# The single-token step of a hybrid decoder layer: eight sequences in one pass, outputs written in place by the products

## The chip, the cores and the metric

The kernel runs on one core of one Trainium2 chip, in one launch. The metric is the device time of the launch in microseconds (us). The time of before is the median of three runs.

## What is computed

Two layers of a decoder. Every layer normalises x, projects it with one large matrix (`w_in`, 3,200 columns in 25 tiles of 128), runs three groups of causal recurrences on the result, gates them and projects back (`w_out`). Two sets of sequences go through the same weights: one prompt of 1,024 tokens, and eight sequences of a single new token each, which bring their own states. The kernel lays both side by side as 1,032 columns (`NT`), the last eight being the single tokens.

The part that concerns us is the single-token step of two of the groups, HGRN2 ("A", six heads, keys of 64) and GLA ("B", six heads, keys of 32), values of 64 each. For every sequence b and head h:

```python
S_new = f[:, None] * S + k[:, None] * v[None, :]   # (K, V)
o     = S_new.T @ q                                # (V,)
```

`S_new` is an output of the kernel, and `o` goes on to a norm over the head, a gate and `w_out`.

## The kernel before

**The large products.** `gemm_tile` (it calls `mm`, L156, the line of every product by `mm`) takes one tile of weights through three blocks of columns (384, 384, 264). Each float32 operand is split into a high and a low part, and each of 8 steps of the contraction makes three products of single-pass type (`wh*hh`, `wh*lo`, `wl*hh`). Weights come in halves of a tile (`raw`, two buffers, 256 KB each, L270 on SyncE's queue), are rounded by ScalarE (`wh`, L146) and subtracted by VectorE or GpSimd in turn (`wl`, L289).

**The rest is woven between them.** Python generators (`unit_a`, `unit_b`, `s5_thread`, `decode` and others) are advanced by `tick()` inside `gemm_tile`; this sets the program order. Tile's scheduler then lays out each engine's order from dependencies and a timeline of its own, when the kernel is built. Each engine, and SyncE's queue (SP), runs its own order strictly: what waits at the head holds up all behind it.

**The single-token step.** `turn` (L856 to L860) transposes the last eight columns of a value tile, ScalarE copies them into `vd` (8 sequences by 128), and a DMA puts them into `vdd` in DRAM, 8 rows of 768. `decode` (L919 to L958) runs five times a layer: B0 (four heads), B1 (two heads, 64 rows), A0, A1, A2 (two heads each), one behind the other by `dec_lock`. A decode

- clears `qbd` (GpSimd, L923) and copies each head's queries into its own column (VectorE, L925);
- in two halves of four sequences: loads the states `dS` (L930) and, one DMA a head, the values broadcast over the head's rows into `dV` (L932); GpSimd makes `dS*f`, `dV*k` and their sum (L935 to L937); SP stores the new states (L939). `dS` has two buffers, `dV` one, so the second half's values are loaded when the first half's sum is done;
- makes eight products with `qbd` as the weights (128x32) and a sequence's states as 64 columns; the outputs lie by sequence and head, so ScalarE copies them to SBUF, TensorE transposes them (L950), ScalarE copies again into `dO`, and two small DMAs a head (64 runs of 16 bytes, L956) carry them to `odec`, rows by head and value.

Each call of `psum("aux")` takes one of two banks that the other threads use too. Much later `dec_norm` reads `odec` (L1377).

What surrounds it on the engines: in `unit_a`, GpSimd multiplies `qs` by `ep` (L985), and VectorE's scans (L874) write over `ep` behind that; `headnorm` on VectorE makes `sl` (L908), on which TensorE waits. In `s5_thread`, GpSimd makes `s5W` (L575 to L580).

Of the kernel before, what the change touches and what calls it, by code (L numbers as in the profile page):

```python
# [8 lines left out]
F32 = mybir.dt.float32  # L9
F32R = mybir.dt.float32r  # L10
I8 = mybir.dt.int8
AF = mybir.ActivationFunctionType
ALU = mybir.AluOpType

P = 128
# [23 lines left out]
def tile_hybrid_step(ctx: ExitStack, tc: tile.TileContext, a: dict, nl=NL, limit=RANGE):  # L39
    nc = tc.nc  # L40
    V, S, G, TE, SY = nc.vector, nc.scalar, nc.gpsimd, nc.tensor, nc.sync

    cst = ctx.enter_context(tc.tile_pool(name="cst", bufs=1))
# [6 lines left out]
    dram = ctx.enter_context(tc.tile_pool(name="dram", bufs=1, space=bass.MemoryType.DRAM))  # L50
# [7 lines left out]
    def nm(s):  # L58
        cnt[0] += 1
        return f"{s}_{cnt[0]}"  # L60
# [16 lines left out]
    def release(x):  # L77
        t = tag_of.pop(id(x))
        del owner[t]
        free.append(t)  # L80

    def psum(tag, shape=(P, 512), dt=F32):
        n = {"g": 2, "att": 1, "o": 2, "aux": 2}[tag]
        return ps.tile(list(shape), dt, tag=tag, bufs=n, name=nm("ps_" + tag))

    def tmp(tag, shape, dt=F32, bufs=1):
        return tp.tile(list(shape), dt, tag=tag, bufs=bufs, name=nm(tag))
# [57 lines left out]
    def act(out, in_, func, **kw):  # L145
        return S.activation(out=out, in_=in_, func=func, **kw)  # L146
# [8 lines left out]
    def mm(out, lhsT, rhs, start=True, stop=True):  # L155
        return TE.matmul(out=out, lhsT=lhsT, rhs=rhs, start=start, stop=stop)  # L156
# [8 lines left out]
    ident = cst.tile([P, P], F32, name="ident")  # L165
# [12 lines left out]
    epsc = cst.tile([P, 1], F32, name="epsc")  # L178
    V.memset(epsc, EPS)
    atts = [cst.tile([P, 2, 2, P], F32, name=f"atts{i}") for i in range(2)]  # L180
    hh = big.tile([P, KD, NT], F32R, name="hh")
    def blocks(dt):

        return [big.tile([P, KD, n], dt, tag=f"lo{b}", name=nm("lo")) for b, (o, n) in enumerate(BLK)]
# [188 lines left out]
    def s5_prep(l, d):  # L373
# [81 lines left out]
        V.tensor_tensor(out=t1, in0=t1, in1=t2, op=ALU.subtract)  # L455
        V.tensor_tensor(out=ci, in0=t1, in1=rd, op=ALU.mult)

        ts = tmp("dV", [P, 4, 64]).rearrange("p a b -> p (a b)")
        bc = lambda x: x.unsqueeze(2).to_broadcast([P, 8, 16])
        cmul(G, bb[:, 0], bb[:, 1], s5w[:, 0], s5w[:, 1], bc(cr), bc(ci), ts[:, :128].rearrange("p (a b) -> p a b", b=16))  # L460
        yield
# [193 lines left out]
    def prep(l):  # L655
        s5["d"] = {}
        s5["th"] = spawn(s5_prep(l, s5["d"]))


    def layer(l, slow=False):  # L660
# [19 lines left out]

        usd = dram.tile([2, P, 8, P], F32, name=nm("usd"))
        udd = dram.tile([2, P, 8], F32, name=nm("udd"))
        vdd = dram.tile([8, 768], F32, name=nm("vdd"))
        st, onorm = {}, {}

        if l == 0:
            masks()
            prep(0)
# [112 lines left out]
        for b in range(3):  # L801
            o, n = BLK[b]
            p = psum("o")
# [5 lines left out]
            x = rbT[:, o:o + n]  # L809
# [27 lines left out]
        def values(w0, part):  # L837
            vt = big.tile([P, 3 * NT], F32, tag=f"vx{part}", name=nm("v"))[:, :3072].rearrange("p (c f) -> p c f", f=384)
            for i in range(3):
                room(1)  # L840
                f = alloc("vf", [P, NT])
                gemm_tile(wt[w0 + i], [0, 1, 2], hrhs, ev_copy(f))
                spawn(turn(vt, f, part, i))
            return vt

        def turn(vt, f, part, i):
            for h in range(2):
                p = psum("aux")
                for c in range(4):
                    t0 = (4 * h + c) * P  # L850
                    TE.transpose(out=p[:, c * P:(c + 1) * P], in_=f[:, t0:t0 + P], identity=ident)  # L851
                act(out=vt[:, 4 * h:4 * h + 4, i * P:(i + 1) * P], in_=p.rearrange("p (c f) -> p c f", f=P),
                    func=AF.Copy)
                yield
            p = psum("aux")
            TE.transpose(out=p[:8, :P], in_=f[:, T:NT], identity=ident)  # L856
            vd = tmp("vd", [8, P])
            act(out=vd, in_=p[:8, :P], func=AF.Copy)
            SY.dma_start(out=vdd[:, part * 384 + i * P:part * 384 + (i + 1) * P], in_=vd)
            release(f)  # L860
            turned[part] += 1


        odec = lay.tile([P, 6, 8], F32, tag="odec", name=nm("odec"))
# [54 lines left out]
        def decode(pr, nh, kd, f8, k8, q8, head0, u0, sin, sout):  # L919

            yield from dec_lock.take()
            qbd = tmp("qbd", [P, 8, 32])[:pr]
            G.memset(qbd, 0.0)  # L923
            for h in range(nh):
                V.tensor_copy(out=qbd[h * kd:(h + 1) * kd, :, h], in_=q8[h * kd:(h + 1) * kd, :])  # L925
            sbs = []
            for b0 in (0, 4):
                sb = tmp("dS", [P, 4, 64], bufs=2)[:pr]
                vb = tmp("dV", [P, 4, 64])[:pr]
                SY.dma_start(out=sb, in_=sin[:, b0:b0 + 4, :])  # L930
                for h in range(nh):
                    SY.dma_start(out=vb[h * kd:(h + 1) * kd], in_=vdd[b0:b0 + 4, (head0 + h) * 64:(head0 + h) * 64 + 64]  # L932
                                 .unsqueeze(0).to_broadcast([kd, 4, 64]))
                yield
                G.tensor_tensor(out=sb, in0=sb, in1=f8[:, b0:b0 + 4].unsqueeze(2).to_broadcast([pr, 4, 64]), op=ALU.mult)  # L935
                G.tensor_tensor(out=vb, in0=vb, in1=k8[:, b0:b0 + 4].unsqueeze(2).to_broadcast([pr, 4, 64]), op=ALU.mult)
                G.tensor_tensor(out=sb, in0=sb, in1=vb, op=ALU.add)  # L937
                yield
                SY.dma_start(out=sout[:, b0:b0 + 4, :], in_=sb)  # L939
                sbs.append(sb)  # L940
            yield

            po = psum("aux")
            for i, sb in enumerate(sbs):
                for b in range(4):
                    mm(po[32 * b:32 * b + 32, 64 * i:64 * i + 64], qbd[:, 4 * i + b, :], sb[:, b, :])
            stg = tmp("dV", [P, 4, 64]).rearrange("p a b -> p (a b)")[:, :P]
            act(out=stg, in_=po[:, :P], func=AF.Copy)
            po = psum("aux")
            TE.transpose(out=po[:, :P], in_=stg, identity=ident)  # L950
            stg = tmp("dO", [P, 4, 4])[:, :nh]
            act(out=stg, in_=po[:, :P].rearrange("p (b h) -> p h b", h=32)[:, :nh], func=AF.Copy)
            for h in range(nh):
                u, hf = divmod(h, 2)
                for i in range(2):
                    SY.dma_start(out=odec[64 * hf:64 * hf + 64, u0 + u, 4 * i:4 * i + 4], in_=stg[64 * i:64 * i + 64, h, :])  # L956
            dec_lock.give()
            decodes[0] += 1  # L958

# [548 lines left out]
    def masks():  # L1508

        for i, m in enumerate((maskA, maskB, maskD)):  # L1510
            mk = tmp("dV", [P, 4, 64]).rearrange("p a b -> p (a b)")[:, :P]
            SY.dma_start(out=mk, in_=a["c_mask"][:, i])
            V.tensor_copy(out=m, in_=mk[:, :m.shape[1]])

# [114 lines left out]
```

## Time and profile before

| | |
|---|---|
| median of the runs | 1073.71 us |
| runs | 1069.07, 1073.71, 1224.8 us |
| the profiled execution, its own time | 1070.87 us |
| its span | 1068.8 us |
| busy: TensorE, VectorE, ScalarE, GpSimd | 94%, 60%, 46%, 44% |
| mean granted TensorE clock | 0.972 of full |

The share of TensorE is high because matmuls are pipelined and the record of each one covers its latency. In the profile's names PE is TensorE, PEld its weight loads, DVE VectorE, ACT ScalarE, POOL GpSimd, SPq the queue from which SyncE issues the DMAs. `<-` names what an instruction waited for last. L156 is the line of the helper that issues every product.

### The profile page before, as it was taken

The page shows a single profiled execution, that of the slowest core. Times are in us where ns is not written, and L with a number is a line of the kernel's source. Part 1 is how long each engine was busy: PE and PEld are TensorE (multiplying, and loading weights), DVE is VectorE, ACT ScalarE, POOL GpSimd, SP SyncE. Part 2 cuts the span into 40 slices and gives each one's busy share as a digit, 9 for nine tenths or more (in the row PEclk, how much of TensorE's full clock was granted, in tenths as well). Part 3 has the DMA queues.
Part 4 walks back from the last instruction along what each step waited for, and adds up shares of the span by engine and source line. Part 5 has one row for each costly group of instructions (what it writes and reads, how often), then busy time and mean ns, then how long its engine had stood idle before and what let it go on. Part 6 is the DMA issues. An engine that isn't in the chain of part 4 may idle for free.

```text
span 1068.8 us, 20962 instructions
## 1 busy us (share of the span) xinstructions
PE 1006.6 (94%) x8071; PEld 946.8 (89%) x8071; DVE 644.8 (60%) x1333; ACT 487.8 (46%) x1001; POOL 466.9 (44%) x668
## 2 busy tenths in 40 slices
PE   6999999999989899999999998999998989999993
PEld 5889987889889799999999997888998989999992
DVE  9985735734656766575474583393478575652345
ACT  7334124376353657634332412245563565763431
POOL 5584664114443545532172267250254363551324
PEclk9899999999989899999999999899999999999997
DMA  7131132121112021134414113112011212112314
GB/s 242 46 104 53 41 93 57 46 60 57 45 37 64 31 82 50 56 121 135 133 45 130 44 42 87 51 41 74 30 50 52 61 46 74 41 60 87 100 43 162
DMA packets 78810, 76.77 MB, mean 72 GB/s; under 512 B 24524, under 2 KB 60652, under 8 KB 78700
## 3 DMA queue, kind: packets, MB, share of 16 engines
q1 hardware_dynamic: 78700, 75.33, 23.1%
q8 instruction: 65, 1.06, 0.4%
q14 instruction: 45, 0.37, 0.1%
HBM read 58.01 MB, written 15.53 MB: 69 GB/s over the span
## 4 chain that ended last, share of the span: by engine, by line
PE 66%; DVE 12%; POOL 10%; DMA 3%; issue 3%; ACT 3%; SPq 2%; DVEq 0%; POOLq 0%; ACTq 0%
PE ps_g L156 52%; PE ps_aux L156 6%; PE ps_o L156 4%; DVE ep L874 2%; PE ps_att L156 2%; DMA dV<-vdd 1%; DMA raw<-in_wf 1%; DVE s5W L584 1%; POOL s5E L365 1%; POOL s5Bm L363 1%; POOL s5E L362 1%; POOL s5Bm L366 1%; POOL s5E L364 1%; PE ps_aux L851 1%; ACT ep L146 1%
## 5 line engine op out<-in xcount | busy, mean ns | idle before, releaser
L156 PE MATMUL ps_g<-hh,wh 128*128 128x384 f32 (+1 forms) x1168 | 384.7, 329 | 1.5 <-DVE qb L742 1.2
L156 PE MATMUL ps_g<-hh,wl 128*128 128x384 f32 (+1 forms) x1168 | 381.4, 327 | 3.5 <-POOL wl L289 3.3
L156 PE MATMUL ps_g<-lo,wh 128*128 128x384 f32 (+1 forms) x1168 | 381.5, 327 | 0.0
L156 PEld LDWEIGHTS ps_g<-hh,wl 128*128 128x128 f32 x1168 | 223.7, 192 | 7.5 <-POOL wl L289 4.3
L156 PEld LDWEIGHTS ps_g<-hh,wh 128*128 128x128 f32 x1168 | 223.6, 191 | 7.5 <-issue 2.6
L156 PEld LDWEIGHTS ps_g<-lo,wh 128*128 128x128 f32 x1168 | 223.8, 192 | 2.6 <-issue 0.8
L289 POOL TENSOR_TENSOR wl<-raw,wh 128x256 fp32r<-128x256 f32 x127 | 107.3, 845 | 262.4 <-ACT wh L146 242.2
L146 ACT ACTIVATE wh<-raw 128x256 fp32r<-128x256 f32 x258 | 102.3, 411 | 134.1 <-PE ps_g L156 115.3
L156 PE MATMUL ps_g<-m,wh 128*128 128x384 f32 (+1 forms) x567 | 136.2, 320 | 0.0
L289 DVE TENSOR_TENSOR wl<-raw,wh 128x256 fp32r<-128x256 f32 x131 | 82.3, 629 | 42.9 <-ACT wh L146 35.0
L156 PEld LDWEIGHTS ps_g<-m,wh 128*128 128x128 f32 x567 | 99.2, 188 | 0.4
L156 PE MATMUL ps_g<-m,wl 128*128 128x384 f32 (+1 forms) x261 | 83.6, 320 | 0.0
L1347 POOL TENSOR_TENSOR z<-z,sg 128x384 f32<-128x384 f32 (+1 forms) x48 | 47.2, 983 | 50.4 <-ACT sg L146 43.1
L156 PEld LDWEIGHTS ps_g<-m,wl 128*128 128x128 f32 x261 | 49.1, 188 | 0.2
L742 DVE TENSOR_TENSOR z<-ps_g,rn 128x384 f32<-128x384 f32 (+1 forms) x48 | 24.4, 509 | 27.9 <-PE ps_g L156 27.9
L146 ACT ACTIVATE sg<-z 128x384 f32<-128x384 f32 (+1 forms) x48 | 23.4, 487 | 29.7 <-DVE z L1345 29.3
L146 ACT ACTIVATE sg<-sg 128x384 f32<-128x384 f32 (+2 forms) x56 | 31.8, 569 | 5.8 <-DVE sg L779 4.8
L156 PE MATMUL ps_g<-vx,wh 128*128 128x384 f32 (+1 forms) x129 | 34.1, 322 | 0.0
L917 DVE TENSOR_TENSOR onorm<-ps_o,sq 128x512 f32<-128x512 f32 x24 | 16.5, 688 | 29.1 <-ACT sq L146 29.1
L1357 DVE SCALAR_TENSOR_TENSOR onorm<-z,vec,onorm 128x384 f32<-128x384 f32 (+1 forms) x36 | 22.0, 614 | 18.9 <-POOL z L1347 18.9
L146 ACT ACTIVATE sg<-sg,ones 128x384 f32<-128x384 f32 (+2 forms) x52 | 32.4, 623 | 0.9
L1436 DVE TENSOR_TENSOR lo<-ps_g,ext 128x384 f32<-128x384 f32 (+1 forms) x24 | 12.3, 512 | 32.9 <-PE ps_g L156 32.8
(385 smaller groups left out, 1846.0 us busy)
## 6 DMA issues: line engine op xcount, KB each, us to landing
raw<-in_wf SPq DMA_DIRECT2D x100, 256.0 KB, 2.8
raw<-in_wo SPq DMA_DIRECT2D x32, 256.0 KB, 3.2
x<-in_xT SPq DMA_DIRECT2D x16, 192.0 KB, 3.8
ext<-in_xT SPq DMA_DIRECT2D x16, 192.0 KB
x1d<-ext SPq DMA_DIRECT2D x16, 192.0 KB, 1.9
ext<-x1d SPq DMA_DIRECT2D x16, 192.0 KB, 2.3
usd<-ucp SPq DMA_DIRECT2D x4, 512.0 KB
s5U<-usd SPq DMA_DIRECT2D x32, 64.0 KB, 2.4
```

The source lines that it names most:

```text
L146: return S.activation(out=out, in_=in_, func=func, **kw)
L156: return TE.matmul(out=out, lhsT=lhsT, rhs=rhs, start=start, stop=stop)
L289: e.tensor_tensor(out=wl, in0=r, in1=wh.bitcast(F32), op=ALU.subtract)
L362: e.tensor_tensor(out=dr, in0=ar, in1=br, op=ALU.mult)
L363: e.tensor_tensor(out=t, in0=ai, in1=bi, op=ALU.mult)
L364: e.tensor_tensor(out=dr, in0=dr, in1=t, op=ALU.subtract)
L742: V.tensor_tensor(out=dst[:, o:o + n], in0=p, in1=rn[:, o:o + n], op=ALU.mult)
L874: V.tensor_tensor_scan(out=g[:, cs], data0=zero[:pr].to_broadcast([pr, ch]) if plus is None else plus[:, cs], data1=x[:, cs], initial=0.0, ...
L917: V.tensor_tensor(out=dst if n < 512 else run(dst), in0=run(po), in1=run(rs), op=ALU.mult)
L1347: G.tensor_tensor(out=z[:, c], in0=z[:, c], in1=sg[:, c], op=ALU.mult)
L1357: V.scalar_tensor_tensor(out=on[:, c], in0=z[:, c], scalar=g, in1=on[:, c], op0=ALU.mult, op1=ALU.mult)
L1436: V.tensor_tensor(out=x, in0=p, in1=xo, op=ALU.add)
```

## The change

All of a decode's eight sequences are done at once. `vdd` becomes head, sequence, value, so the values of a head are one run of 2 KB, and one DMA broadcasts them over the rows of all heads of a decode. The states are one load, one buffer (`dS` and `dV` both grow from 4 to 8 sequences), one store. The three GpSimd operations take 512 elements a row in place of 256. `qbd` is made by one VectorE operation from the queries and a constant of ones and zeros (`rows_of`, made once at the start by GpSimd). The products swap operands: a sequence's states are the weights (128 rows, 64 columns), the queries of the even or of the odd heads the one or two columns that stream; the outputs land with values as rows, in the upper or lower half, as `odec` wants them. One ScalarE copy puts them there. The transpose, the second copy and the small DMAs are gone. The count of `yield` goes from five to four.

```diff
+    rows_of = {64: cst.tile([P, 2, 1], F32, name="rows64"), 32: cst.tile([P, 2, 2], F32, name="rows32")}
+    for kd, x in rows_of.items():
+        G.memset(x, 0.0)
+        for h in range(P // kd):
+            G.memset(x[h * kd:(h + 1) * kd, h % 2, h // 2:h // 2 + 1], 1.0)
...
-        vdd = dram.tile([8, 768], F32, name=nm("vdd"))
+        vdd = dram.tile([12, 8, 64], F32, name=nm("vdd"))
...
-            SY.dma_start(out=vdd[:, part * 384 + i * P:part * 384 + (i + 1) * P], in_=vd)
+            h = 6 * part + 2 * i
+            SY.dma_start(out=vdd[h:h + 2].rearrange("h b v -> b h v"), in_=vd.rearrange("b (h v) -> b h v", v=64))
...
-            qbd = tmp("qbd", [P, 8, 32])[:pr]
-            G.memset(qbd, 0.0)
-            for h in range(nh):
-                V.tensor_copy(out=qbd[h * kd:(h + 1) * kd, :, h], in_=q8[h * kd:(h + 1) * kd, :])
-            sbs = []
-            for b0 in (0, 4):
-                sb = tmp("dS", [P, 4, 64], bufs=2)[:pr]
-                vb = tmp("dV", [P, 4, 64])[:pr]
-                SY.dma_start(out=sb, in_=sin[:, b0:b0 + 4, :])
-                for h in range(nh):
-                    SY.dma_start(out=vb[h * kd:(h + 1) * kd], in_=vdd[b0:b0 + 4, (head0 + h) * 64:(head0 + h) * 64 + 64]
-                                 .unsqueeze(0).to_broadcast([kd, 4, 64]))
...
-            po = psum("aux")
-            for i, sb in enumerate(sbs):
-                for b in range(4):
-                    mm(po[32 * b:32 * b + 32, 64 * i:64 * i + 64], qbd[:, 4 * i + b, :], sb[:, b, :])
-            stg = tmp("dV", [P, 4, 64]).rearrange("p a b -> p (a b)")[:, :P]
-            act(out=stg, in_=po[:, :P], func=AF.Copy)
-            po = psum("aux")
-            TE.transpose(out=po[:, :P], in_=stg, identity=ident)
...
-                    SY.dma_start(out=odec[64 * hf:64 * hf + 64, u0 + u, 4 * i:4 * i + 4], in_=stg[64 * i:64 * i + 64, h, :])
+            nu = nh // 2
+            sb = tmp("dS", [P, 8, 64])[:pr]
+            vb = tmp("dV", [P, 8, 64])[:pr]
+            SY.dma_start(out=sb, in_=sin)
+            SY.dma_start(out=vb, in_=vdd[head0:head0 + nh].rearrange("h b v -> h (b v)").unsqueeze(1).to_broadcast([nh, kd, 512]))
+
+            qbd = tmp("qbd", [P, 2, 2, 8])[:pr, :, :nu]
+            V.tensor_tensor(out=qbd, in0=q8.unsqueeze(1).unsqueeze(1).to_broadcast([pr, 2, nu, 8]),
+                            in1=rows_of[kd][:pr, :, :nu].unsqueeze(3).to_broadcast([pr, 2, nu, 8]), op=ALU.mult)
+            yield
+            yield
+            G.tensor_tensor(out=sb, in0=sb, in1=f8.unsqueeze(2).to_broadcast([pr, 8, 64]), op=ALU.mult)
+            G.tensor_tensor(out=vb, in0=vb, in1=k8.unsqueeze(2).to_broadcast([pr, 8, 64]), op=ALU.mult)
+            G.tensor_tensor(out=sb, in0=sb, in1=vb, op=ALU.add)
+            yield
+            SY.dma_start(out=sout, in_=sb)
+            yield
+
+            p = psum("aux")
+            po = p[:, :8 * nu].rearrange("p (u b) -> p u b", b=8)
+            for b in range(8):
+                for hf in range(2):
+                    mm(po[64 * hf:64 * hf + 64, :, b], sb[:, b, :], qbd[:, hf, :, b])
+            act(out=odec[:, u0:u0 + nu, :], in_=po, func=AF.Copy)
```

## Rows read from the trace of the kernel before

**Rows 1.** The page: busy us, share of the span and instructions by engine.
```profile
PE 1006.6 (94%) x8071; PEld 946.8 (89%) x8071; DVE 644.8 (60%) x1333; ACT 487.8 (46%) x1001; POOL 466.9 (44%) x668
```

**Rows 2.** Waits of all engines: waiter <- waited for: us, times, longest us.
```profile
POOL dV L936 <- DMA dV<-vdd: 38.1, 15, 5.1
...
PE ps_aux L156 <- DVE sl L908: 10.5, 3, 5.1
```

**Rows 3.** Waits of PE alone, the same columns.
```profile
PE ps_aux L156 <- DVE onorm L1046: 3.4, 1, 3.4
PE ps_g L156 <- POOL wl L289: 3.3, 2, 1.9
```

**Rows 4.** Timeline of POOL, A1's decode in layer 0, second half: start us, us [idle before].
```profile
302.51 0.61 POOL L936 TENSOR_TENSOR dV<-dV,k 128x256 f32<-128x256 f32 x1 [4.04 <-DMA dV<-vdd]
303.20 0.73 POOL L937 TENSOR_TENSOR dS<-dS,dV 128x256 f32<-128x256 f32 x1
303.89 2.48 POOL L985 TENSOR_TENSOR qs<-qs,ep 128x512 f32<-128x512 f32 x2
```

**Rows 5.** Timeline of SP's queue in the same stretch.
```profile
291.69 2.52 SPq L956 DMA_DIRECT2D odec<-dO  x4
294.26 0.62 SPq L932 DMA_DIRECT2D dV<-vdd  x1
```

**Rows 6.** Timeline of DVE, just behind that.
```profile
305.19 1.33 DVE L874 TENSOR_TENSOR_SCAN ep<-zero,s 128x64 f32<-128x64 f32 x1 [5.20 <-POOL qs L985]
306.44 0.66 DVE L908 TENSOR_TENSOR sl<-sq,sh 128x512 fp32r<-128x512 f32 x1
```

**Rows 7.** Windows: stretch: us, busy us by engine, PEclk, DMA share of 16 engines, GB/s.
```profile
303.50:307.20 3.70, 0.10 (x1) 0.00 (x0) 2.02 (x3) 0.00 (x0) 2.87 (x3) 0.85 0.11 38
307.30:312.90 5.60, 5.60 (x22) 5.40 (x23) 5.05 (x22) 1.92 (x4) 1.80 (x1) 0.50 0.00 0
...
187.10:188.90 1.80, 0.25 (x4) 0.06 (x1) 1.80 (x4) 0.22 (x1) 1.02 (x3) 1.00 0.04 1
190.20:193.40 3.20, 3.20 (x11) 2.69 (x10) 3.20 (x10) 0.00 (x0) 0.00 (x0) 0.50 0.00 0
```

**Rows 8.** Timeline of SP's queue, B1's decode in layer 0.
```profile
166.98 3.02 SPq L956 DMA_DIRECT2D odec<-dO  x5
170.10 1.00 SPq L932 DMA_DIRECT2D dV<-vdd  x2
```

**Rows 9.** Timeline of POOL, what follows the same decode.
```profile
179.48 1.28 POOL L575 TENSOR_TENSOR s5W<-s5V,s5E 128x512 f32<-128x512 f32 x1
```

**Rows 10.** Timeline of POOL, A2's decode in layer 0, between its halves.
```profile
340.18 2.52 POOL L985 TENSOR_TENSOR qs<-qs,ep 128x512 f32<-128x512 f32 x2
```

**Rows 11.** Timeline of DVE, A0's decode in layer 1.
```profile
782.28 2.42 DVE L925 COPY qbd<-q 64x8 f32<-64x8 f32 x2
```

**Rows 12.** Windows, as in Rows 7: a load whose source begins with 6; a 256 KB load.
```profile
203.30:206.10 2.80, 2.80 (x20) 2.55 (x19) 2.06 (x6) 0.00 (x0) 0.00 (x0) 1.00 0.77 267
549.34:550.14 0.80, 0.80 (x6) 0.80 (x5) 0.80 (x3) 0.00 (x0) 0.80 (x2) 1.00 0.37 92
```

**Rows 13.** Tile dV: time of its DMAs from issue to landing.
```profile
DMA to landing us min/median/max: 1.7/2.0/2.3
```

**Rows 14.** Timeline of PE: a decode's products and transpose, and products of weights 128x64.
```profile
376.22 0.43 PE L156 MATMUL ps_aux<-dS,qbd 128*32 128x64 f32 x16
376.58 0.44 PE L156 MATMUL ps_g<-lo,wh 128*128 128x384 f32 x1
...
380.30 0.33 PE L950 MATMUL ps_aux<-ident,dV 128*128 128x128 f32 x1
380.56 0.66 PE L156 MATMUL ps_o<-qs,Sp 64*64 64x64 f32 x8
...
163.64 0.68 PE L156 MATMUL ps_aux<-s5U,s5Bm 128*64 128x136 f32 x8
164.26 0.39 PE L156 MATMUL ps_g<-hh,wl 128*128 128x264 f32 x1
```

## The prediction on record

> **What bounds the kernel now.** Read the busy shares first, then who waits for whom, then the stretches in which TensorE stands. TensorE is busy 94% of the span, 62 us short of all of it [rows 1]. So no more than those 62 us can be won, less what the start and the end of the kernel need, unless TensorE itself gets less to do, and this change gives it more. The step that is changed does not bound the kernel by its own work; it counts where it makes another engine late on which TensorE then waits. The list of waits names the candidate: GpSimd stood 38.1 us in 15 waits for the values' load, the longest 5.1, in a queue in which everything else of GpSimd stands behind it [rows 2]. One such case can be followed. In A1's decode of layer 0 GpSimd waits 4.04 us for the second half's values, makes the product and the sum, and only then reaches `qs*ep` at 303.89 [rows 4]. VectorE's scan stood 5.20 us for that, and `sl` stands behind the scan [rows 6]. TensorE waits for `sl`: 3.6 of the 3.7 us from 303.5 are empty [rows 7]. Then comes a second bill: right behind this idle stretch the granted clock is 0.50 for 5.6 us, the lower level (1.2 GHz), which loses about half of them, 2.8 us [rows 7]. Behind the smaller gap before 188.9 (1.55 us empty) it is 0.50 for 3.2 us, so 1.6 us lost [rows 7]. A gap that closes is thus worth about twice its length. TensorE's waits for `sl` are 10.5 us in three [rows 2], for `onorm` 3.4 us, and for weights (`wl`) 3.3 us in two [rows 3]. Some 15 us of waits, with their clock perhaps 25, are in reach of the change. A change of 2%, 21 us, is about what a measurement of this kernel can tell from none.
>
> **The change part by part.** The sum is made against the profiled execution's own 1070.87 us, 2.8 under the median of the runs shown, 1073.71.
>
> *The second round.* Today the second half's values can be asked for only when the first half's sum is done, so 2.0 us of landing [rows 13] and the issues lie bare in every decode, with GpSimd at the head of its queue. That goes. GpSimd's own work stays: six operations of 0.61 to 0.73 us [rows 4] become three of some 1.28 us, the time of 512 elements a row [rows 9], so 3.9 us against 3.9; the clearing of `qbd` is saved as well.
>
> *The small DMAs.* SP issued 48 of them over the run (two a head, twelve heads a layer, two layers): four took 2.52 us [rows 5], in front of the next value load. In B1 the last five alone held the queue 3.02 us before the values went out at 170.10 [rows 8]. They go, and so do the ten transposes and ten copies on ScalarE; ScalarE bounds nothing here. The write of `vdd` in more, shorter runs costs nothing I can see: hundreds of microseconds or other decodes lie between most writes and their use, and where they don't, it is one DMA as now.
>
> *The new value load.* Its source begins with the heads, two or four, and then repeats each for 64 or 32 rows. No load of before has that form with two; the nearest is one whose source begins with six. While it ran, 0.37 of 16 engines were busy, 5.9 of them [rows 12]. So I take the outermost count to be the number of engines: two for A and B1, four for B0. A 256 KB load ran at 267 GB/s on 0.77 of 16, 21.7 GB/s an engine [rows 12]. A's 256 KB (128 rows of 2 KB) on two engines then take 6.0 us, B0's and B1's 3.0; over sixteen it would be 0.7. With the 2.0 us of landing [rows 13] that is 8.0 us for A and 5.0 for B, bounds 2.7 and 8.0. I take the long ends.
>
> *Where that leaves GpSimd.* A1 of layer 0: with one load of states and one of values the values' issue is over near 291.2, they land at 299.2, product and sum (1.28 and, scaled from 0.73, 1.4 us) end at 301.8: `qs*ep` starts 2.1 us sooner than 303.89. The gap shrinks from 3.6 to 1.5 us, and the slow clock behind it from 5.6 to 3.2 us as behind the other gap of that size [rows 7], which is worth 1.2: **-3.3 us**. B1 of layer 0: the values go out near 164 instead of 170, land at 169, and GpSimd is through near 172, where today it starts `s5W` at 179.48 [rows 9]. The gap of 1.55 us before 188.9 closes with its 1.6 of clock: **-3.1 us**. What is late next there is VectorE, whose work stays. A2 of layer 0: here `qs*ep` stands between the two halves, at 340.18 [rows 10]. Now it stands behind the whole decode or in front of it. Behind it, the load is up to 6 us longer, against an issue that no longer waits for the decode before to give `dV` back. Bounds: 7.4 us later (8.0+1.3+1.4 against 2.0+0.6+0.7) and none; I take **+2 us**, near the low end, because the issue moves up by most of the difference.
>
> *The queries.* Each head's copy by VectorE goes, one operation comes. In A0 of layer 1 the two copies took 2.42 us [rows 11], in front of the scans and, later, of the `onorm` for which TensorE waits 3.4 us [rows 3]. One small operation at 0.2 us: **-2.2 us**, bounds 0 and 3.4. Elsewhere such copies lie in VectorE's slack.
>
> *TensorE.* The old products take 0.36 us of its time (376.22 to 376.58, 16 records, 22 ns each), the transpose 0.26 us [rows 14]. The new ones are 16 with two records each, 32 weight loads of 64 columns, each followed by one or two streaming columns. At the old pace they take 0.7 us. At that of the products whose weights have this shape (eight records in 0.62 us, 77 ns, with 136 columns streaming) they take 2.5 us [rows 14]. I take 45 ns, 1.45 us, the middle: the weights are of the second row's size, the stream of less than the first's. That is +0.8 us a decode, bounds +0.1 and +1.9, and +8 us over ten (+1 to +19). TensorE waits soon after in about half of the decodes, where this is hidden until that wait closes; paid in five: **+4 us**.
>
> The Trainium skill (TensorE: Matmul & The Clock Gate, LDWEIGHTS) prices a weight load at its columns over 1.2 in ns, whatever streams behind it. By that figure it is an estimate of 53 ns, 1.7 us a decode and +11 us over ten in place of +8. No row shows a load of 64 columns with so short a stream.
>
> Two things are priced at nothing. The second bank of `aux` is held for a shorter time, which the waits of TensorE above do not show as their end. And the whole order is laid out anew, a shift of a few us of either sign.
>
> Sum: -3.3 - 3.1 + 2 - 2.2 + 4 = -2.6. **1070.87 - 2.6 = 1068.3 us.**
>
> **The rivals.**
>
> *The values land fast (faster).* If the load spreads over sixteen engines, it lands in 2.7 us, `qs*ep` in A1 and A2 comes five or more us sooner, and all gaps close: A1 3.6+2.8, A2 5.1 [rows 2] and 2.8 for its clock (estimated like A1's), B1 3.1, A0 3.4, in all 20.8 us, less 1 to 4 for the products: 1052 to 1054. For it: the loads of today land in 2.0 us. Against it: the 0.37 of [rows 12]. The skill's page on DMA: Bandwidth & Descriptors (Why a DMA increments its semaphore by 16 and not by 1) speaks against it too: the engines used are the largest number up to 16 that divides the outermost counts of both sides, here two or four.
>
> *The change does not do what it says.* The second round goes, but its wait comes back as one long wait: nothing won in A1 and A0. Left are -3.1+2+4: 1073.8. For it: 8.0 us is as long as both rounds' landings with their issues.
>
> *TensorE pays (slower than before).* At 77 ns a record and none of it hidden the products add 19 us; with B1's gain and A2's loss, 1070.87+19-3.1+2 = 1089. It decides from a pace of about 47 ns on with all ten paid, where ten times 0.9 us eats the 8.6 us of gains. For it: TensorE's 94%. Against: it is hidden where a wait follows.
>
> *Weights come late (slower by over 2%).* A weight half uses all sixteen engines, so a value load that holds two of them for 6 us delays a half that is issued behind it. Six such loads are 36 us; TensorE pays only what the lead of the weights doesn't cover. Half of it would be 18, with +8 of products 1097. Against it: in the whole run TensorE waits 3.3 us for weights [rows 3].
>
> **How the numbers follow.** Forecast (1062 to 1072) 0.42; fast landing 0.20; no gain (1072 to 1078) 0.16; TensorE pays (1078 to 1090) 0.15; weights late 0.07. Range 1051 to 1088: it takes in the forecast, no gain, and most of fast landing and of TensorE pays. Faster by over 2% (under 1052): 0.08, a good third of the fast landings. Slower by over 2% (over 1095): 0.08, the late weights and the tail of TensorE pays. Within 2%: 0.84.
>
> **What would show it.** GpSimd's waits for the values' load: ten or fewer, near 20 us in all. Value loads of A on two engines: DMA share near 0.13 where nothing else runs. The gap before `s5W`'s products in layer 0 gone, that of A1 halved, and the slow clock behind them with them. Thirty-two records of a decode in 1.45 us. Wrong it would be if TensorE waits for `wl` by more than 10 us, if the values land in under 3 us, or if 32 records take 2 us and more.

## The result, and the profile after

The changed kernel takes 1087.54 us (median; 1086.24 to 1089.13), the kernel before beside it 1071.57: a ratio of 1.0148, 95% interval 1.0132 to 1.0165. That is 16 us slower, where 5 us faster than the median shown was forecast. (One of the four runs of the kernel before, 1224.8 us, fell in a slower state; the median has it, the ratio leaves it out.) The time lies just inside the stated range, 1051 to 1088, but it is slower and not faster. The first lines of the page of after, to be held against [rows 1]:

```profile
span 1084.8 us, 20997 instructions
## 1 busy us (share of the span) xinstructions
PE 1018.4 (94%) x8221; PEld 960.6 (89%) x8221; DVE 642.3 (59%) x1319; ACT 479.7 (44%) x985; POOL 449.8 (41%) x636
```

VectorE, ScalarE and GpSimd all have less to do than before. Only TensorE has more, 11.8 us by the page, in which the slower clock is counted too. The waits of TensorE (engine, tile, line, what it waited for: us in all, times, longest), beside [rows 2, 3]:

```profile
PE ps_o L156 <- DVE Sp L905: 6.7, 3, 5.0
PE ps_aux L156 <- DVE sl L915: 6.6, 3, 2.9
...
PE ps_aux L156 <- DVE kst L537: 5.4, 3, 3.1
...
PE ps_g L156 <- DVE wl L295: 2.4, 1, 2.4
```

`sl` fell from 10.5 to 6.6 us, `onorm` is gone from the top, but the state scan `Sp` and `kst` have come up. GpSimd's list no longer has a row `dV <- vdd` (38.1 us before).

Where is it lost? The 4752 large products come in nearly the same order in both, so the time at the n-th of them can be compared. At product 2850, 640 us in, well behind layer 0's step, after is 1.7 us behind; at the last one it is 16.3 behind. So some 15 us are lost in layer 1. The stretch behind product 2850, before and then after (stretch: its length, busy us of TensorE, its weight loads, VectorE, ScalarE and GpSimd, granted clock, DMA share, GB/s):

```profile
635.60:1049.30 413.70, 401.40 (x3414) 379.56 (x3413) 229.45 (x428) 203.82 (x408) 168.04 (x203) 0.98 0.21 62
```

```profile
637.40:1065.70 428.30, 407.86 (x3489) 386.67 (x3487) 228.34 (x424) 200.97 (x401) 158.49 (x185) 0.96 0.20 59
```

There TensorE stands idle for 20.4 us in place of 12.3, and its granted clock is 0.96 in place of 0.98. Shorter windows of after show how:

```profile
300.00:312.00 12.00, 11.63 (x164) 11.24 (x165) 6.01 (x11) 4.83 (x6) 6.05 (x7) 1.00 0.29 93
...
705.00:710.00 5.00, 2.87 (x22) 2.43 (x20) 5.00 (x14) 1.72 (x3) 0.30 (x1) 1.00 0.00 0
...
711.00:718.00 7.00, 7.00 (x39) 5.88 (x38) 5.58 (x13) 3.11 (x6) 2.09 (x3) 0.57 0.01 1
...
820.00:830.00 10.00, 5.03 (x70) 4.70 (x68) 9.84 (x22) 0.74 (x2) 2.64 (x3) 0.73 0.16 57
...
840.00:850.00 10.00, 10.00 (x114) 9.17 (x113) 3.08 (x8) 4.95 (x8) 1.04 (x1) 1.00 0.11 36
...
870.00:880.00 10.00, 5.41 (x120) 4.56 (x118) 9.89 (x15) 5.50 (x12) 7.21 (x6) 0.96 0.01 2
880.00:890.00 10.00, 8.39 (x61) 8.06 (x62) 5.21 (x11) 7.53 (x18) 2.47 (x3) 0.70 0.16 53
```

The first row is A1 of layer 0: the idle stretch and slow clock of [rows 7] are gone, as forecast (by another path, as the last part shows). The others are layer 1. VectorE is full (5.00 of 5, 9.84 and 9.89 of 10) while TensorE stands for half the time; behind or within each such stretch the clock is at its lower level for a part (0.57, 0.73, 0.70); twenty microseconds on, VectorE is nearly idle (3.08 of 10). It is the same work, bunched. What stands in front on VectorE near 820 (start, duration, engine, line, operation):

```profile
820.04 1.04 DVE L1042 TENSOR_TENSOR onorm<-ps_aux,ac 128x512 f32<-128x512 f32 x1
820.91 3.49 DVE L881 TENSOR_TENSOR_SCAN ep<-ep,s 128x64 f32<-128x64 f32 x13
824.33 2.26 DVE L905 TENSOR_TENSOR_SCAN Sp<-Sp,onorm 128x1024 f32<-128x1024 f32 x1
```

Thirteen decay scans of A1, whose result is needed later, stand ahead of A0's state scan, for which TensorE waits 4.97 us:

```profile
826.64 3.57 PE L156 MATMUL ps_o<-qs,Sp 64*64 64x64 f32 x60 [4.97 <-DVE Sp L905]
```

In the kernel before, the state scan came first:

```profile
809.18 2.62 DVE L898 TENSOR_TENSOR_SCAN Sp<-Sp,onorm 128x1024 f32<-128x1024 f32 x1
...
812.29 3.78 DVE L874 TENSOR_TENSOR_SCAN ep<-ep,s 128x64 f32<-128x64 f32 x16
```

A sum over TensorE's records (each interval from start to start is split into the time of its columns, what the lower clock adds, and idle time beyond 0.1 us) gives after against before: idle +4.9, lower clock +4.5, the decodes' products and transposes +5.9 (3.3 to 9.2), the rest +0.7; together 16.0.

### The profile page after: what moved, and what is told of

The parts are those of the page before. It is cut to its first block, busy times and chain, and to the rows that moved or that the text cites. A ratio compares the mean times of both kernels' runs of the same rounds, so it can differ in the third digit from the quotient of the medians.

```text
span 1084.8 us, 20997 instructions
## 1 busy us (share of the span) xinstructions
PE 1018.4 (94%) x8221; PEld 960.6 (89%) x8221; DVE 642.3 (59%) x1319; ACT 479.7 (44%) x985; POOL 449.8 (41%) x636
## 3 DMA queue, kind: packets, MB, share of 16 engines
q8 instruction: 66, 1.08, 0.4%
## 4 chain that ended last, share of the span: by engine, by line
PE 63%; DVE 16%; POOL 9%; issue 4%; ACT 4%; DMA 2%; SPq 1%; DVEq 0%; POOLq 0%; ACTq 0%
PE ps_g L156 49%; PE ps_aux L156 6%; PE ps_o L156 4%; DVE ep L881 2%; ACT ep L146 2%; DVE s5W L590 2%; PE ps_att L156 2%; DMA ysd<-s5Y 1%; POOL s5E L370 1%; POOL s5E L371 1%; SPq L649 1%; DVE Sp L905 1%; POOL s5Bm L369 1%; DVE lo L223 1%; POOL s5Bm L372 1%
## 5 line engine op out<-in xcount | busy, mean ns | idle before, releaser
L156 PEld LDWEIGHTS ps_g<-hh,wh 128*128 128x128 f32 x1168 | 225.0, 193 | 15.3 <-issue 4.9
L1353 DVE SCALAR_TENSOR_TENSOR onorm<-z,vec,onorm 128x384 f32<-128x384 f32 (+1 forms) x36 | 24.6, 685 | 28.2 <-POOL z L1343 28.2
L1432 DVE TENSOR_TENSOR lo<-ps_g,ext 128x384 f32<-128x384 f32 (+1 forms) x24 | 12.3, 513 | 33.2 <-PE ps_g L156 33.1
L146 ACT ACTIVATE sq<-ps_aux,epsc 128x512 f32<-128x512 f32 x24 | 16.4, 683 | 34.6 <-PE ps_aux L156 34.5
```

The lines of the kernel that those rows point to most:

```text
L1353: V.scalar_tensor_tensor(out=on[:, c], in0=z[:, c], scalar=g, in1=on[:, c], op0=ALU.mult, op1=ALU.mult)
L1432: V.tensor_tensor(out=x, in0=p, in1=xo, op=ALU.add)
```

## Experiments

In the tables "by 2850" and "behind" are the time against the kernel before (profiled executions) lost up to large product 2850 and after it, that is in layers 0 and 1. Each rests on one execution, and they vary without any change of order: after, a_fs and a_fss run layer 0 in the same order on every engine and show +1.7, +3.3 and +6.8 there; so do m_new0y, m_p1 and m_h1, with -7.7, -0.1 and -6.1. A difference of 5 to 8 us in one of these columns is therefore no finding by itself; where a time with its interval bears on the point, it decides.

**1. Work that doesn't change.** One yield more in the changed decode; one fewer in the old; the old kernel with the eight clears of the constant, which nothing reads.

```diff
 # a_y5, changed decode, ahead of its products
+            yield
 # b_y4, old decode, ahead of its products
-            yield
 # b_rows, old kernel, at the start
+    rows_of = {...}; G.memset(...) x8
```

> The changed kernel with a fifth yield in the decode, as before had five: no work, no operand and no wait is other, only the point in program order at which the products are issued. Order theory (the 16 us are lost because the new decode makes the scheduler lay all engines' orders anew, worse in layer 1): it moves by 5 us or more from 1087.5, either way. Work theory (products, weights or the small VectorE operation cost them): 1085 to 1090. Blocked-operation theory (the 16-element product for qbd stands 1.1 us on VectorE behind GpSimd's qs*ep in all six A decodes): 1085 to 1090.

> The kernel before with one yield less in the decode (four, as the changed kernel): the same work. Order theory: it moves by 5 us or more from 1071.6, either way. Work theory and blocked-operation theory: 1069 to 1074.

> The kernel before with the two constants of the change made at the start and used by nobody (eight small clears on GpSimd more). Order theory: it may move by a few us, 1065 to 1082. Work theory and blocked-operation theory: 1069 to 1074, since eight clears at the start are under 2 us of an engine that waits there.

| | us | ratio to before | by 2850 | behind |
|---|---|---|---|---|
| after | 1087.5 | 1.0132 to 1.0165 | +1.7 | +14.6 |
| a_y5 | 1099.9 | 1.024 to 1.0296 | +15.3 | +10.9 |
| b_y4 | 1073.7 | 0.9986 to 1.0034 | -1.5 | +1.3 |
| b_rows | 1079.4 | 1.0034 to 1.0083 | +5.3 | +2.9 |

A yield that issues nothing costs the changed kernel 12 us, the old one none; eight clears of 0.1 us cost the old one some 6 (interval 3.6 to 8.9). So the laid order alone is worth up to a dozen microseconds. That is more than the "few" that the forecast allowed it.

**2. The queries' operation.** In the changed kernel, VectorE's product of 16 elements a row (L936) takes this long (engine, operation, count: ns least/median/most):

```profile
L936 DVE TENSOR_TENSOR qbd<-q,rows x10: 141/1083/1178, 120.2 to 857.9; 128x16 f32<-128x16 f32 x6, 128x32 f32<-128x32 f32 x2, 64x16 f32<-64x16 f32 x2
```

In all six decodes of A it runs while GpSimd multiplies `qs` by `ep`, as here, VectorE's row and GpSimd's (idle time before it in brackets):

```profile
857.88 1.08 DVE L936 TENSOR_TENSOR qbd<-q,rows 128x16 f32<-128x16 f32 x1
...
857.65 2.53 POOL L981 TENSOR_TENSOR qs<-qs,ep 128x512 f32<-128x512 f32 x2 [4.36 <-ACT ep L146]
```

```diff
-            V.tensor_tensor(out=qbd, ...
+            G.tensor_tensor(out=qbd, ...
```

> The changed kernel with the small product for qbd on GpSimd instead of VectorE, so that VectorE no longer stands 1.1 us behind qs*ep in each A decode. Blocked-operation theory: 1087.5 less 6 to 10, so 1077 to 1082. Work theory (the products on TensorE): 1084 to 1089. Order theory: anything from 1068 to 1095, with the gaps of TensorE in layer 1 at other places.

Measured: 1081.45 us, 1.0069 to 1.0124; by 2850 -2.9, behind +13.4. GpSimd does it in 0.22 us (median; 2.20 in one of the six). The kernel is 6 us faster, clear of noise, but that isn't six decodes of one microsecond. Counted by large products, a_qG gains its lead of 5 us on after in one stretch of layer 0, from 156 to 198 us, in which no decode of A stands; the three decodes of A in layer 0 gain it some 0.4 us, the three in layer 1 at most 2. What differs in that stretch is TensorE's clock. Windows of after, then of a_qG:

```profile
187.00:192.80 5.80, 4.89 (x28) 3.97 (x26) 5.80 (x8) 0.83 (x2) 3.37 (x3) 1.00 0.02 5
192.80:200.00 7.20, 7.20 (x43) 6.17 (x42) 7.20 (x25) 2.35 (x6) 0.81 (x2) 0.53 0.00 0
```

```profile
183.30:189.10 5.80, 4.89 (x27) 3.93 (x26) 5.80 (x8) 0.77 (x2) 3.31 (x3) 1.00 0.01 4
189.10:196.30 7.20, 6.39 (x59) 5.67 (x58) 7.20 (x25) 2.29 (x6) 1.03 (x2) 1.00 0.01 1
```

In both TensorE waits 0.91 us before `sl`. Behind it the clock falls to its lower level in after and stays at 1.00 in a_qG. So the operation on VectorE is worth some 2 us by the trace, and why the clock fell in the one and not in the other stays open.

**3. VectorE's order in layer 1, put right by hand.** A dependency puts A1's decay scans behind A0's state scan (a_fs; VectorE's row of large steps differs from after's in that alone); a second puts the S5 scans behind the normalisation (a_fss); a_rV has only the clears on VectorE; a_all has everything, and the queries' operation on GpSimd.

```diff
+                if l and ch == 64:
+                    behind(i, last_states)   # decay scan behind the state scan
+                    if l:
+                        behind(x, last_on)   # S5 scan behind headnorm's product (a_fss, a_all)
```

> The changed kernel with one order forced: in layer 1, a head pair's decay scans (VectorE) must come behind the state scan of the pair before. In the laid order of VectorE's large steps this is the only difference: 32 decay scans and then the state scan become 16, the state scan, 16, as in the kernel before. No work is added or removed. Order theory (the loss sits in layer 1, where VectorE does another unit's scans ahead of one on which TensorE waits): the 5.1 us that TensorE waits for this scan near 826.6 go, and up to 3 us of the half clock around it: 3 to 8 us less than the changed kernel's 1087.5, so 1080 to 1085. Work theory (the changed operations themselves cost the time): 1086 to 1089, as nothing of them is changed. Blocked-operation theory (the queries' operation stands behind GpSimd's large product): also 1086 to 1089, since that is as before.

> As the run with one forced order, and a second: in layer 1 the S5 scans must come behind the last normalisation's product that was issued ahead of them. In VectorE's laid order the eight scans of the second S5 block then stand in one row behind two normalisations, where the changed kernel puts four between the square's low part and the product. Order theory: the 3.0 us wait near 710.7 and the 6.8 us of half clock behind it go as well, another 3 to 7 us, so 1074 to 1081. But S5's results then come some 10 us later; if TensorE comes to wait for them it is 1080 to 1090. Work theory and blocked-operation theory: 1086 to 1089.

> The changed kernel with the eight clears for the constant of ones and zeros made by VectorE at the start, not by GpSimd. If the 4.8 us lost by product 450 come from these clears standing at the head of GpSimd's queue: that is won, 3 to 6 us, and the later order is laid anew (it takes on one of the two orders of before in layer 1: 16 decay scans, the state scan, 16), another 3 to 8 us; together 1074 to 1082. If the early loss has another cause: 1080 to 1085 from the order of layer 1 alone. Work theory: 1086 to 1089.

> The changed kernel with all repairs: both forced orders in layer 1, the clears at the start on VectorE, the queries' operation on GpSimd. Order theory together with the blocked operation: 4.8 (start) + 4 (queries) + 5 + 5 (the two orders) less than 1087.5: 1066 to 1072, that is level with the kernel before or up to 5 us faster, since what the change saves in layer 0 then shows. Work theory: not under 1080, since the products, the loads and GpSimd's operations are the changed kernel's.

| | us | ratio to before | by 2850 | behind |
|---|---|---|---|---|
| a_fs | 1089.3 | 1.0112 to 1.0194 | +3.3 | +16.9 |
| a_fss | 1081.7 | 1.0058 to 1.0107 | +6.8 | +6.6 |
| a_rV | 1085.0 | 1.0064 to 1.0164 | +3.3 | +10.0 |
| a_all | 1077.9 | 1.0035 to 1.0076 | -6.4 | +11.0 |

The first order won nothing: 1089.3 is at the end of what the expectation gave to the theory that it called work (1086 to 1089), not to that of order (1080 to 1085). Its wait was handed on (timeline of TensorE in a_fs: the scan, then the mask behind it, idle time before each in brackets):

```profile
824.71 3.57 PE L156 MATMUL ps_o<-qs,Sp 64*64 64x64 f32 x60 [2.51 <-DVE Sp L909]
836.51 1.99 PE L156 MATMUL ps_o<-atts,v 64*64 64x64 f32 x64 [2.72 <-DVE atts L1078]
```

2.51 and 2.72 in place of 4.97: VectorE's queue is full there, and in this run another step is late in its place. The second order won 6 us: the wait of 2.79 us for `sl` at 710.66 in after has no counterpart in a_fss, where the wait for `Sp` is still 3.67. The clears on VectorE alone (a_rV) gave no gain clear of noise. All repairs together came to 1077.9, 10 us better than after. That is 6 short of the 1066 to 1072 expected by the one theory, and under the 1080 that the other set as the least, so it decides for neither.

**4. Which layer.** m_new0x has the changed step in layer 0 alone (clears on VectorE, queries on GpSimd), m_new1 in layer 1 alone, the other layer the old one.

```diff
+        decode = decode_new if l == 0 else decode_old   # m_new0x; l == 1: m_new1
```

> The changed single-token step in layer 0 alone (with the clears at the start on VectorE and the queries' operation on GpSimd); layer 1 has the old step in two halves, with its queries' tile and its buffers cut out of the new, larger ones. If the loss belongs to the changed step in layer 1's phase A (there the run with all repairs lost 21 us against the kernel before, after being 6.5 us ahead at the end of layer 0's step): the lead of layer 0 stays, 1064 to 1069. If the loss is only the spread of laid orders, whatever step they are laid around: anywhere from 1064 to 1085, and layer 1 loses again, though its step is the old one.

> The reverse: the old step in layer 0, the changed one in layer 1 alone (clears at the start on GpSimd and queries on VectorE, as in the changed kernel). In VectorE's laid order, layer 1 has the changed kernel's row: four S5 scans between the square's low part and the product, and 32 decay scans ahead of the first pair's state scan. If the loss is of layer 1: 1082 to 1090. If it is of the whole order and not of this layer: 1070 to 1082.

m_new0x: 1067.36 us, 0.9935 to 0.9967, by 2850 -5.0, behind -1.3. m_new1: 1089.9 (its runs spread from 1080 to 1095), 1.0069 to 1.021, +5.7 and +18.8. The loss goes with the changed step in layer 1; the changed step in layer 0 alone beats both kernels. Its page:

```profile
span 1062.4 us, 20981 instructions
## 1 busy us (share of the span) xinstructions
PE 1004.4 (95%) x8146; PEld 945.9 (89%) x8146; DVE 647.3 (61%) x1329; ACT 482.7 (45%) x992; POOL 464.8 (44%) x653
```

**5. Orders laid without the scheduler's timeline.** Both kernels, the changed one with five yields; the order then comes from the program and its dependencies.

```diff
-    with _tile.TileContext(nc, schedule_with_timeline_sim=True) as tc:
+    with _tile.TileContext(nc, schedule_with_timeline_sim=False) as tc:
```

> The changed step, with as many yields as before (five), laid out by the scheduler without its own timeline, so that no estimated time enters the order; to be read against the kernel before laid in the same manner (next run). Order theory: against that kernel the change is then worth what its operations are worth, from 10 us faster (GpSimd's waits go) to 4 slower (TensorE's products); the absolute time may be anything from 1060 to 1200. Work theory: again some 15 us slower than that kernel.

> The kernel before, laid out without the scheduler's timeline: the partner of the run above. Alone it shows how much the order is worth: order theory 10 us or more away from 1071, since the large products wait for what stands first on the other engines; if the order hardly matters, within 5 us of 1071.

Old step 1135.5 us (1133.9 to 1138.3), changed step 1139.1 (1137.4 to 1140.6): 3.6 us apart, not 16. The old kernel, laid without the timeline, takes 64 us more. The 3.6 is no clean price of the change's own operations: both kernels wait so much more here that a loss can hide in the waits or be added to. The pair also shows what a small delay does. Up to 98 us VectorE has the same 212 instructions in the same order in both; TensorE's product at 82.75 us in the old comes 0.9 us later in the changed one. Windows of the old, then of the changed kernel:

```profile
80.00:85.00 5.00, 3.92 (x25) 3.45 (x25) 5.00 (x16) 2.91 (x6) 5.00 (x2) 1.00 0.17 57
85.00:90.00 5.00, 5.00 (x33) 4.91 (x32) 3.36 (x10) 1.08 (x4) 1.94 (x4) 1.00 0.29 65
```

```profile
80.00:85.00 5.00, 3.31 (x15) 2.78 (x15) 5.00 (x15) 2.53 (x6) 5.00 (x2) 0.80 0.16 53
85.00:90.00 5.00, 5.00 (x19) 4.90 (x19) 3.23 (x11) 1.14 (x3) 2.06 (x3) 0.52 0.22 53
```

0.6 us less of TensorE's work before 85 us, and the clock falls to its lower level where it had stayed at 1.00: the delay of 0.9 us has become 3.7 by 90 us.

**6. Which half of the change, and the start.** By product 450 (113 us) after was 4.8 us behind, and the clears were suspected. a_late asks for them at the first decode; m_new0y is m_new0x with that; m_new0z has no constant at all. In layer 1 m_p1 has the one pass with the old products and small DMAs, m_h1 the two halves with the new products (both with m_new0y's layer 0). m_new0zy is m_new0z with a yield more in layer 1's old decode.

```diff
 # a_late, m_new0y: at the head of the changed decode
+            make_rows()
 # m_new0z: ones from a constant that is there already
+                                in1=obd32[:pr, ::64]....to_broadcast([pr, 2, nu, 8]), op=ALU.mult)
 # m_p1, layer 1: SY.dma_start(out=sb, in_=sin) ... mm(po[32 * b:32 * b + 32, ...], qbd[...], sb[...])
 # m_h1, layer 1: for b0 in (0, 4): ...      ... mm(po[64 * hf:64 * hf + 64, :, b], sbs[...], qbd[...])
```

> The changed kernel with the constant of ones and zeros made at the first decode (some 150 us in) by GpSimd, not at the start. If the 4.8 us lost by product 450 of the large products (about 115 us in) come from the eight clears: this kernel stands with the kernel before there (within 1 us), and the whole is some 4 us less plus what the new order gives, 1077 to 1085. If they have another cause (with the clears on VectorE the loss by product 450 was 7.2 us, with them on GpSimd 4.6 to 4.8): it loses 4 to 7 us there again, and the whole is 1083 to 1090.

> The changed step in layer 0 alone, the old one in layer 1, the queries' operation on GpSimd, as in the run at 1067.4, but with the constant made at the first decode. If the clears at the start cost: 1062 to 1066; if they cost nothing of their own: 1066 to 1070. The kernel before stands at 1072.

> As the run before (changed step in layer 0), with layer 1's step taking the loads and GpSimd's operations of the change (all eight sequences at once), but the old products, transpose, copies and small DMAs; the queries' tile, for want of room, is cut out of the values' tile and filled after the sum. If layer 1's loss comes from the one pass (GpSimd through sooner, or with longer operations): 1076 to 1084. If it comes from the products with the states as weights: 1062 to 1069, as with the old step.

> The reverse in layer 1: the old two halves with their loads and GpSimd's operations, but the new products, with the queries' operation and one copy. If layer 1's loss comes from the products (or from the place that the scheduler gives them in the order): 1074 to 1084. If it comes from the one pass: 1062 to 1069. If both are near 1072, the loss is of neither part by itself.

> The changed step in layer 0 alone, the old one in layer 1, and no constant of ones and zeros: for the units of 64 rows a head the queries' operation (GpSimd) takes its ones from a constant that the kernel has, for B0 GpSimd clears and copies. So GpSimd has one clear at its start, as the kernel before, and not nine. If the 4.4 to 5 us lost by product 450 come from the eight clears: they are back, and it is 1060 to 1065. If they come from the order laid anew: it stays at 1064 to 1068. The kernel before is at 1072.

> As the run beside it, with one yield more in layer 1's old step, ahead of its products: work that does not change. If layer 1's loss (10 to 15 us with the one pass there, with the new products there, or with both) is what any disturbance of the laid order costs: 5 us or more slower than the run beside it, lost after product 3000. If it belongs to the change's own operations: within 3 us of the run beside it.

| | us | ratio to before | by 2850 | behind |
|---|---|---|---|---|
| a_late | 1081.1 | 1.007 to 1.01 | -2.0 | +13.2 |
| m_new0y | 1066.1 | 0.9936 to 0.9968 | -7.7 | +4.0 |
| m_p1 | 1081.0 | 1.0048 to 1.0096 | -0.1 | +16.6 |
| m_h1 | 1076.2 | 1.003 to 1.0071 | -6.1 | +11.2 |
| m_new0z | 1069.0 | 0.9954 to 0.9999 | +0.8 | +2.7 |
| m_new0zy | 1068.3 | 0.9954 to 1.0 | -1.8 | -2.2 |

The suspicion fell. The scheduler put a_late's clears back to 2.5 to 4.1 us, and m_new0z, without any, is 4.2 us behind at product 450 all the same. So a_late is no test of late clears; with the same operations as after and the clears some 2 us later, it is a third laid order of the same work, and 6 us faster than after. By product 600 (151 us) after and every kernel of this group are within some 1 us of before. The lead of before was lost again: between products 450 and 600 it waits for `wl` and has the lower clock for a part. Windows of before, then of after:

```profile
113.10:150.50 37.40, 35.31 (x242) 31.52 (x241) 21.59 (x49) 8.46 (x18) 28.45 (x57) 0.98 0.23 69
```

```profile
117.90:151.50 33.60, 33.60 (x242) 30.93 (x241) 16.80 (x33) 8.40 (x19) 26.57 (x55) 1.00 0.24 73
```

In layer 1, with either half of the change there, or both, 6.6 to 18.8 us are lost (eleven kernels laid with the timeline); with the old step there, -2.2 to +4.0 (six kernels, a yield more or fewer and the idle clears among them). The gap of 2.6 us between the two groups is smaller than what one execution varies by, and the times overlap: 1076.2 to 1099.9 for the first group, 1066.1 to 1079.4 for the second. Either half thus makes a loss likely, and no more than that is shown. (The buffers alone are not the cause: in the m_new0 kernels the old step takes its halves out of the new, larger buffers and loses nothing.)

Whether the laid order alone does it in layer 1, or the change's own operations have a part, is not settled. By its recorded expectation m_new0zy, which loses nothing, speaks for the operations. But its yield moves only 14 of some 445 VectorE instructions of layer 1, where the yield of a_y5 moved 86; b_y4 (70) and b_rows (49) are the better controls, and they lose little too. m_p1 differs from m_new0y in more than its half: it takes the queries' tile out of that of the values and fills it after the sum, with a yield more. Against the operations alone speak after, a_late and a_y5: the same work takes 1087.5, 1081.1 and 1099.9 us.

## Why the forecast was wrong, point by point

- **The step that failed** is the last term, "the whole order is laid out anew, a shift of a few us of either sign", priced at nothing. The sum thus had waits of A and B that close, and none that opens. In layer 1 the new kernel lost 14.6 us: TensorE stands idle 8 us more and has the lower clock longer, in waits for VectorE that before doesn't have (4.97 us for `Sp`, 2.79 and 2.94 for `sl`). In the pair of experiment 5, 3.1 us were lost there (+3.9 at the last product, +0.8 at 2850), so some 11.5 us, as an estimate, go with the laid order; that rests on a pair that is no clean price. Part is shown: the same work in other laid orders spans 1081 to 1100 us, putting back one order won 6 us, another nothing. Why layer 1's order is worse with either half of the change stays open, and so does how much of the loss the change's own operations make there.
- **The second round** was right in kind and better than forecast. GpSimd's waits for the values are 0 us, not 20: its operations stand far behind the loads. A1's load of values in layer 0 is issued at 263.58, when A0's sum has left the buffer, and GpSimd's first operation on it comes at 288.74, 25 us later. For that reason the length of the load, on which two rivals hung, decided nothing. (For the states' loads GpSimd still waits 7.7 us in two waits, before 9.6 in four.) The load itself came as priced. In [rows 12] the row of 0.77 is the 256 KB load and the row of 0.37 the load whose source begins with 6; the prediction reads them so. This window lies inside A1's load, with two of sixteen engines and 50 GB/s:

```profile
268.00:270.00 2.00, 2.00 (x13) 2.00 (x12) 2.00 (x2) 0.07 (x1) 2.00 (x2) 1.00 0.13 50
```

  128 packets of 2 KB at a median of 84 ns on two engines are 5.4 us, where 6.0 was the estimate. The page DMA: Bandwidth & Descriptors of the Trainium skill (the engines used divide the outermost counts) agrees with this row.
- **A1 of layer 0**: the idle stretch closed wholly, not to 1.5 us, but not because GpSimd came to `qs*ep` sooner. `qs*ep` starts later than before (310.04; 303.89 before), held up by ScalarE and not by the values:

```profile
310.04 2.55 POOL L981 TENSOR_TENSOR qs<-qs,ep 128x512 f32<-128x512 f32 x2 [5.88 <-ACT ep L146]
```

  In front of the product of `sl` TensorE now has 1134 large products, 1125 before. So GpSimd is no longer late by the values, as forecast, but the stretch closed with the help of the laid order. A2's wait for `sl` (5.1 us in [rows 2]), priced as a loss of 2, closed as well. **B1**: TensorE's wait before `sl` is still 0.91 us, and a longer slow clock stands behind it (0.53 from 192.8 to 200.0, shown in experiment 2, against 3.2 us at 0.50 in [rows 7]). That -3.1 did not come.
- **The queries**: "one small operation at 0.2 us" was 1.08 to 1.18 us in each decode of A, where it stands beside `qs*ep`. The row to see it in was there: the two copies of 2.42 us [rows 11], which met the same neighbour. The 2.2 us won in A0 are not shown: its wait of 3.4 us for `onorm` in layer 1 is gone, but one of 0.95 stands there.
- **TensorE's products**: 32 records take 1.03 us from the first to the next other product, not 1.45:

```profile
679.81 1.10 PE L156 MATMUL ps_aux<-qbd,dS 128*64 128x2 f32 x32
680.84 0.45 PE L156 MATMUL ps_g<-hh,wh 128*128 128x384 f32 x1
```

  Counted as the prediction counts, a decode's products and transpose took 0.62 us before [rows 14], so a decode costs some 0.4 us more, and ten cost +4 where the prediction had +8 before hiding. The sum paid +4, half of them; that size comes out if none is hidden. (The sum over TensorE's records above has 9.2 against 3.3, +5.9; it counts each record to the start of the next and leaves out the time behind the last of a decode.) By the Trainium skill (TensorE: Matmul & The Clock Gate, LDWEIGHTS) one load of 64 columns is 53 ns as an estimate. The records come in pairs, one product for each half of the output's rows: 7 ns apart in a pair, some 58 ns from one pair to the next. So the trace agrees for a pair, and shows that the second load of a pair adds little here: 32 loads take 1.03 us and not the 1.7 of the prediction's estimate by the page.
- **The rivals**: the time is that of "TensorE pays" (1089), by another mechanism: its pace of 77 ns did not come. "Weights late" did not come either; TensorE's waits for `wl` come to 4.0 us (2.4 for VectorE's, in the row shown above, and 1.6 for GpSimd's), before 3.3.

Layer 0 taken alone doesn't settle the forecast. Its terms with half of TensorE's 4 say -2.4 there. The six kernels with the change as forecast in layer 0 (queries on VectorE) stand at -2.0 to +15.3 by product 2850, +4.7 in the mean; the eight with the queries' operation on GpSimd at -7.7 to +0.8, -3.7 in the mean. That the second group lies near -2.4 is luck as far as the terms go: A1's gain came by another path, A2's loss and B1's gain did not come.

## What to carry to other kernels

Where a scheduler lays the order from its own timeline, an edit is priced with the order that it brings: price the new order as a term of its own, with the spread that edits without work show (here 0 to 12 us), and try the edit layer by layer, since the one layer may win and the other lose. Look for what the saved wait lets go ahead: on a queue that is full, like VectorE's in layer 1, earlier work pushes in front of the step for which TensorE waits, and putting one step back may hand the wait on, as in a_fs, or win, as the second order did in a_fss. Before a gain is put down to the work that was moved, see by the trace whether it arises where that work stands: in a_qG most of it did not.

## What the runs showed of the hardware

A VectorE product of 16 or 32 elements a row takes 0.14 to 0.18 us in the four decodes of B. With 16 it takes 1.08 to 1.18 us in the six decodes of A, beside a GpSimd operation of 512 elements a row, and ends within 0.03 us of the end of the first such operation that it started beside (at 858.96 and 858.93 for the row shown). On GpSimd itself it takes 0.21 to 0.23 us in five of six decodes of A, and 2.20 in the sixth, beside a VectorE scan of 1024 elements a row. In one pair of runs a delay of 0.9 us of one product came with TensorE's lower clock behind it and grew to 3.7 us; in another pair the same wait of 0.91 us stood in both, and the clock fell in one alone.
